# A hybrid decoder block on one core: norms taken by positions, a last sum moved ahead of scalings, and seven operand tiles loaded earlier

## The chip, the cores and the metric

The kernel runs on one core of a Trainium2 chip. The metric is the device time of one execution in microseconds (us), as the median of several runs. The engines of the core work beside each other, each through its own list of instructions in order: TensorE (PE in the profile; PEld is its loading of weights), VectorE (DVE), ScalarE (ACT), GpSimd (POOL), and SyncE (SP), which here only issues DMA transfers. Matmul results land in PSUM, where the kernel keeps eight buffers (banks) of 128 x 512 fp32.

## The reference

One layer of a decoder over 2048 positions and 1024 channels: a norm, an input projection, two mixers beside each other (gated linear attention and a short gated convolution), an output projection with a residual sum, a second norm, a gated FFN with 2816 inner channels and a residual sum, and a final norm. What the change touches are the second and the final norm and the end of the FFN:

```python
def rmsnorm(x, g):
    xf = x.astype(jnp.float32)
    y = xf * lax.rsqrt(jnp.mean(xf * xf, axis=-1, keepdims=True) + NORM_EPS)
    return (y * g.astype(jnp.float32)).astype(x.dtype)
...
        x = x + mixed
        h2 = rmsnorm(x, norm2_g[l])
        ffn = (jax.nn.silu(h2 @ w_ffn_gate[l]) * (h2 @ w_ffn_up[l])) @ w_ffn_down[l]
        x = x + ffn
    return rmsnorm(x, norm_f_g)
```

## The kernel before

**Layout.** Activations lie with channels on the 128 partitions and positions along the free dimension. The 2048 positions are four blocks of 512 (`PB`); two blocks, `j` = 0 and 1, form a half, and the kernel goes through the layer in two halves. 1024 channels are eight tiles (`d` or `k`). A tile is 128 x 512 fp32.

**Products.** fp32 accuracy is had from fp32r matmuls: `split` (L145 and L146) writes the rounded part of a tile on ACT and the rest of it on DVE, and `product_step` (L358 to L360) makes three matmuls for each pair of tiles. `unit` multiplies a 2 x 2 arrangement of blocks with seven products instead of eight (`PRODUCTS`); its weights are combined on POOL (L341 to L348) and split; its results are copied out of PSUM on ACT (L378) and added on DVE (L382). Operand pairs (`op`, 512 KB) lie in a pool `opp` of 28 buffers, raw weights in a pool of two, tiles of work beside the products in a pool of 11 (`bt`), split tiles on their way to DRAM (`so`) in a pool of 3.

**FFN.** For each half `ffn_up` runs over 11 pairs of row tiles: gate and up products, silu, product, and the split operands are stored to DRAM (`sa_...`) by a background generator. Then `ffn_down` sums over the 11 pairs in four groups (`GROUPS`: 2, 3, 3 and 3 pairs). For each group it loads 14 or 21 operand pairs (`act_op`, L137 on SP) and runs four units, each for two output tiles. The sums `y` of group 0 lie in 7 buffers of `opp`. The last unit of the second half is `last_unit`: four plain blocks of 18 matmuls, one for each of two tiles and two blocks of positions.

**Norms.** The sum of squares over the eight tiles is kept as a tile `ssq` of 128 x 512. `column_rstd` (L163) or `psum_rstd` (L170) multiplies it with a 128 x 128 matrix of ones, in plain fp32, so that every partition has the total (`tot`, PSUM). `finish_rstd` takes Ln (L176) and Exp (L177) on ACT, and one Newton step on DVE: L178, and L155 to L157 through `newton`. Scaled tiles follow on DVE (L482, L965, L992). ACT loads a table of functions when it goes from silu to Ln, from Ln to Exp, and back. There are eight such norms: two of the first half, taken while the second half's output projection runs (`h2_first`, near 714 us), two of the second half, taken beside the first half's `ffn_up` (`h2_ahead`, near 821 and 844), two final norms of the first half beside the second half's `ffn_up` (`finish_later`, near 1551 and 1730), and two at the end (`norm` in `last_unit`, L983 and L984, with the last tile's squares `q` as a second matmul).

**The end.** `last_unit` adds the last products to the sums (L1009), takes squares (ACT L1011), multiplies by the gains (L978), takes `norm(0)` ahead of the last 18 matmuls and `norm(1)` behind them, and scales block 0, then block 1 (L992): six tiles of each on DVE, two (`d` = 2 and 5) on POOL, which works from a copy of the norm in SBUF made by ACT (L986). Each scaled tile is stored (SP, L140).

**What sets the order.** The program is written once, in the order of the Python code; a planner with simulated times then fixes each engine's list when the kernel is built. `background` generators add norm and split work between products (`tick`). On the chip each engine keeps its list, whatever comes late.

## Time and profile before

| | |
|---|---|
| median of 3 runs | 2129.43 us (2121.35 to 2132.37) |
| profiled execution | 2130.55 us |
| its span | 2128.8 us |
| mean granted TensorE clock | 0.987 |
| PE busy | 2043.5 us, 96% |
| DVE, ACT, POOL busy | 1415.6, 1015.7, 971.7 us |
| DMA | 470.74 MB, mean 221 GB/s |

A line of the waits has the waiting engine, its instruction, what released it, and then the total in us, the number of waits and the longest. A line of the timeline has start, length, engine, source line and operation, output and inputs, a count where equal instructions are merged, and in brackets the idle time before it and what ended it. A line of the windows has the stretch, its length, the busy time and number of instructions of PE, PEld, DVE, ACT and POOL (or of one engine alone), then the granted clock, the DMA engines' share and GB/s. Where a tile or line is asked for, a line has the count, the shortest, median and longest duration in ns, and the first and last start. A line of the page's groups ends with busy time, mean ns and idle time before.

### The profile page before, as it was taken

The numbers are of one execution on the slowest core, as the hardware profiler recorded it, in microseconds if no ns is written. First come the engines' busy times: TensorE is split into PE (matmuls) and PEld (weight loads), VectorE is DVE, ScalarE is ACT, GpSimd is POOL, SyncE is SP. The second block draws the span as 40 slices with busy tenths as digits, with TensorE's granted clock in tenths as the row PEclk, the third lists the DMA queues.
The fourth block names the chain that finished last, engine by engine and source line by source line (L and its number), as shares of the span: only waits on it lengthen the run. The fifth ranks groups of instructions, "written<-read, shape, count | busy, mean of one in ns | idle before, by whom it ended". The sixth has DMA issues, their size and how long they took to land.

```text
span 2128.8 us, 26931 instructions
## 1 busy us (share of the span) xinstructions
PE 2043.5 (96%) x9133; PEld 1653.7 (78%) x9133; DVE 1415.6 (66%) x1983; ACT 1015.7 (48%) x1997; POOL 971.7 (46%) x703
## 2 busy tenths in 40 slices
PE   5999999999999999999999999999999989999996
PEld 4777787887888888788888877787888878886774
DVE  7668765549753695887886655654766666664554
ACT  5555445656543345545545443333554454453344
POOL 3435322222102464565464437864545545435774
PEclk9999999999999999999999999999999999999998
DMA  7349586424586872655646677697454535587662
GB/s 272 127 149 310 189 337 216 144 100 133 183 302 219 333 275 99 238 198 212 224 168 217 256 304 262 239 343 291 158 211 170 208 129 187 203 330 268 266 267 109
DMA packets 190971, 470.74 MB, mean 221 GB/s; under 512 B 20016, under 2 KB 65264, under 8 KB 181232
## 3 DMA queue, kind: packets, MB, share of 16 engines
q1 hardware_dynamic: 190832, 469.01, 60.6%
q8 instruction: 72, 1.18, 0.2%
q14 instruction: 67, 0.55, 0.1%
HBM read 300.63 MB, written 168.30 MB: 220 GB/s over the span
## 4 chain that ended last, share of the span: by engine, by line
PE 76%; DMA 10%; DVE 8%; ACT 3%; issue 2%; POOL 0%; SPq 0%; DVEq 0%; ACTq 0%; POOLq 0%
PE mm L358 22%; PE mm L360 22%; PE mm L359 21%; PE mm L776 2%; PE mm L777 2%; PE mm L779 2%; DMA raw<-in_wdown_dram 2%; DVE wq L146 2%; DMA op<-sa_T 1%; DMA op<-sa_B 1%; DMA op<-shT 1%; DVE so L146 1%; DVE op L146 1%; DMA h<-in_xt_dram 1%; DVE h L482 1%
## 5 line engine op out<-in xcount | busy, mean ns | idle before, releaser
L358 PE MATMUL mm<-op,wq 128*128 128x512 f32 x2499 | 985.4, 396 | 29.1 <-ACT c L378 9.8
L360 PE MATMUL mm<-op,wq 128*128 128x512 f32 x2499 | 970.4, 393 | 14.9 <-DVE wq L146 14.0
L359 PE MATMUL mm<-op,wq 128*128 128x512 f32 x2499 | 979.2, 392 | 0.0
L146 DVE TENSOR_TENSOR wq<-raw,wq 128x512 fp32r<-128x512 f32 (+2 forms) x626 | 524.6, 844 | 334.0 <-ACT wq L145 332.1
L145 ACT ACTIVATE wq<-raw 128x512 fp32r<-128x512 f32 (+2 forms) x626 | 364.8, 587 | 588.3 <-PE mm L360 421.2
L358 PEld LDWEIGHTS mm<-op,wq 128*128 128x128 f32 x2499 | 472.5, 189 | 147.8 <-ACT c L378 13.1
L360 PEld LDWEIGHTS mm<-op,wq 128*128 128x128 f32 x2499 | 472.5, 189 | 126.5 <-DVE wq L146 27.1
L359 PEld LDWEIGHTS mm<-op,wq 128*128 128x128 f32 x2499 | 472.9, 189 | 97.0 <-issue 1.0
L343 POOL TENSOR_TENSOR raw<-s,raw 128x512 f32<-128x512 f32 (+2 forms) x97 | 127.2, 1311 | 437.2 <-DVE wq L146 416.6
L382 DVE TENSOR_TENSOR c<-mm,c 128x512 f32<-128x512 f32 x267 | 182.8, 685 | 113.2 <-PE mm L360 109.9
L341 POOL TENSOR_TENSOR s<-raw 128x512 f32<-128x512 f32 (+2 forms) x97 | 127.3, 1313 | 196.5 <-DMA raw<-in_wffn_dram 90.3
L348 POOL TENSOR_TENSOR raw<-raw 128x512 f32<-128x512 f32 (+2 forms) x97 | 125.9, 1298 | 137.0 <-DVE wq L146 129.8
L378 ACT ACTIVATE c<-mm 128x512 f32<-128x512 f32 x267 | 154.4, 584 | 26.4 <-PE mm L360 23.9
L758 POOL TENSOR_TENSOR ssx<-ssx,q 128x512 f32<-128x512 f32 x52 | 76.2, 1477 | 159.8 <-ACT q L757 159.6
L342 POOL TENSOR_TENSOR raw<-raw 128x512 f32<-128x512 f32 (+2 forms) x97 | 136.8, 1411 | 4.4
L938 POOL TENSOR_TENSOR y<-c,y 128x512 f32<-128x512 f32 x66 | 99.1, 1504 | 68.9 <-DVE c L382 68.7
L146 DVE TENSOR_TENSOR so<-t,so 128x512 fp32r<-128x512 f32 x100 | 90.8, 914 | 19.0 <-ACT so L145 18.7
L145 ACT ACTIVATE wq<-s 128x512 fp32r<-128x512 f32 (+2 forms) x97 | 56.8, 586 | 92.7 <-PE mm L360 90.7
L776 PE MATMUL mm<-op,wq 128*128 128x512 f32 x256 | 100.9, 395 | 0.0
L777 PE MATMUL mm<-op,wq 128*128 128x512 f32 x256 | 99.8, 390 | 0.0
L146 DVE TENSOR_TENSOR wq<-s,wq 128x512 fp32r<-128x512 f32 (+2 forms) x97 | 86.1, 887 | 16.0 <-ACT wq L145 15.3
L145 ACT ACTIVATE so<-t 128x512 fp32r<-128x512 f32 x100 | 62.5, 628 | 44.2 <-DMA sa_B<-so 17.5
(175 smaller groups left out, 1882.2 us busy)
## 6 DMA issues: line engine op xcount, KB each, us to landing
raw<-in_wffn_dram SPq DMA_DIRECT2D x44, 1024.0 KB, 5.9
sa_T<-so SPq DMA_DIRECT2D x88, 512.0 KB, 5.0
op<-sa_T SPq DMA_DIRECT2D x88, 512.0 KB, 9.6
sa_B<-so SPq DMA_DIRECT2D x69, 512.0 KB, 3.4
op<-sa_B SPq DMA_DIRECT2D x69, 512.0 KB, 9.6
raw<-in_win_dram SPq DMA_DIRECT2D x23, 1024.0 KB, 5.3
raw<-in_wdown_dram SPq DMA_DIRECT2D x24, 768.0 KB, 6.1
sx<-y SPq DMA_DIRECT2D x48, 256.0 KB, 3.1
```

The source lines that it names most:

```text
L145: last_hi[:] = [act.activation(hi, src, AF.Copy)]
L146: return dve.tensor_tensor(lo, src, hi.bitcast(F32), ALU.subtract)
L341: pool.tensor_tensor(s1, a21, a22, ALU.add)
L342: pool.tensor_tensor(a21, a11, a21, ALU.subtract)
L343: pool.tensor_tensor(a11, s1, a11, ALU.subtract)
L358: pe.matmul(o[:], wh, xh, start=first and k == 0, stop=False, skip_group_check=True)
L359: pe.matmul(o[:], wh, xl, start=False, stop=False, skip_group_check=True)
L360: return pe.matmul(o[:], wl, xh, start=False, stop=k == n - 1, skip_group_check=True)
L378: act.activation(t[:], o[:], AF.Copy)
L382: dve.tensor_tensor(t[:], o[:], t[:], ALU.add)
L776: pe.matmul(o[e, j][:], wh, m[:, 0, :], start=k == 0, stop=False)
L777: pe.matmul(o[e, j][:], wh, m[:, 1, :], start=False, stop=False)
```

## The change

Three things change.

1. The norms after the first one go by positions (`position_rstd`). `ssq` becomes the stationary side of four matmuls with one column of ones, so that the totals of 512 positions come out as 128 x 4 in PSUM (`rs`). DVE computes the reciprocal root from a bit trick and three Newton steps on 128 x 4 elements, all without ACT; a copy on DVE spreads it to 128 x 512 (`rep`), and four transposes on PE give the row that every partition needs (`rb_ps`). At the end a second set of transposes goes to a bank of its own, for ACT's copy. Ln, Exp and their table loads go; `ident` moves to a pool that lives to the end.
2. At the end the last sum and its squares come ahead of block 0's scalings on DVE. Block 0's tiles 2, 5 and 6 go to POOL, 0 and 1 to DVE after the last sum, 3, 4 and 7 to DVE after the second norm's copy.
3. In `ffn_down`, seven (`EARLY`) of the 21 operand pairs of group 1 are loaded in the second unit of group 0, by the program's order, instead of after group 0.

```diff
-    ident = mixer.tile([P, P], F32, name="ident")
+    ident = const.tile([P, P], F32, name="ident")
...
-    def column_rstd(ssq, n, rb=None):
-    def psum_rstd(ssq, n):
-    def finish_rstd(v, tot, n, rb=None):
...
+    def position_rstd(n, *sums, into=()):
+        s, rb = bank("rs"), bank("rb_ps")
+        tot, v, l = [s[:, i * PT : (i + 1) * PT] for i in range(3)]
+        y = tiny.tile([P, PT], F32, name="py", tag="py")[:]
+        for t in range(PT):
+            for i, ssq in enumerate(sums):
+                pe.matmul(
+                    tot[:, t : t + 1], ssq[:, t * P : (t + 1) * P], one_t, start=i == 0,
+                    stop=i == len(sums) - 1,
+                )
+        dve.tensor_scalar(v, tot, 1.0 / n, EPS, ALU.mult, ALU.add)
+        li = l.bitcast(I32)
+        dve.tensor_scalar(li, v.bitcast(I32), 1, None, ALU.arith_shift_right)
+        dve.tensor_scalar(y.bitcast(I32), li, -1, 0x5F3759DF, ALU.mult, ALU.add)
+        for _ in range(3):
+            dve.tensor_tensor(l, v, y, ALU.mult)
+            dve.scalar_tensor_tensor(l, l, -0.5, y, ALU.mult, ALU.mult)
+            dve.scalar_tensor_tensor(y, l, 1.5, y, ALU.add, ALU.mult)
+        rep = bt("rep", (P, PT, P))
+        last_rep[:] = [
+            dve.tensor_copy(rep[:], y.rearrange("p (t c) -> p t c", c=1).to_broadcast([P, PT, P]))
+        ]
+        for dst in (rb, *into):
+            for t in range(PT):
+                pe.transpose(dst[:, t * P : (t + 1) * P], rep[:, t, :], ident[:])
         return rb
...
-            column_rstd(ssq[j], D, rb[j])
+            act.activation(rb[j][:], position_rstd(D, ssq[j])[:], AF.Copy)
...
-            rb.append(psum_rstd(ssq[j], D))
+            rb.append(position_rstd(D, ssq[j]))
...
+        def group_op(m, n):
+            return early.pop((m, n)) if (m, n) in early else act_op(half, m, n)
...
+                if u == 0 and d0 == 2:
+                    order = [(m, n) for _, n in PRODUCTS for m in range(GROUPS[1], GROUPS[2])]
+                    for m, n in order[:EARLY]:
+                        early[m, n] = act_op(half, m, n)
...
-            act.preload_act_table_set("natural_log_exp_and_others")
-            rb = psum_rstd(ssq, D)
+            rb = position_rstd(D, ssq)
...
         def norm(j, q):
-            tot, rb = bank("tot"), bank("rb")
-            pe.matmul(tot[:], ones[:], ssq[j][:], start=True, stop=False)
-            pe.matmul(tot[:], ones[:], q[:], start=False, stop=True)
-            finish_rstd(ssq[j], tot, D, rb)
-            act.activation(ssq[j][:], rb[:], AF.Copy)
+            copied = bank("rb_ps")
+            rb = position_rstd(D, ssq[j], q, into=[copied])
+            act.activation(ssq[j][:], copied[:], AF.Copy)
             return rb
...
-                dve.tensor_tensor(yy, o[:], yy, ALU.add)
+                added = dve.tensor_tensor(yy, o[:], yy, ALU.add)
...
                 if j and not r:
-                    rbs.append(norm(0, q[0]))
-        rbs.append(norm(1, q[1]))
-        for j in range(2):
-            scale(j, rbs[j])
+                    rb = norm(0, q[0])
+                    for d in (2, 5, 6):
+                        scale(0, d, None)
+        for d in (0, 1):
+            with tc.issue_after(added.ins):
+                scale(0, d, rb)
+        rb1 = norm(1, q[1])
+        for d in (3, 4, 7):
+            with tc.issue_after(last_rep[0].ins):
+                scale(0, d, rb)
+        for d in range(KD):
+            scale(1, d, None if d in (2, 5) else rb1)
```

More of the change, by code (lines that the diff above doesn't have):

```diff
@@ L13 @@
 U32 = mybir.dt.uint32
+I32 = mybir.dt.int32
 AF = mybir.ActivationFunctionType
@@ L30 @@
 LAST_GROUP = GROUPS[-1]
+EARLY = 7
 EPS = 1e-6
@@ L157, in newton @@
         dve.scalar_tensor_tensor(y, l, 1.5, y0, ALU.add, ALU.mult)
-    def column_rstd(ssq, n, rb=None):
-        rb = ssq if rb is None else rb
-        tot = bank("tot")
-        pe.matmul(tot[:], ones[:], ssq[:], start=True, stop=True)
-        finish_rstd(rb, tot, n)
-        return rb
-    def psum_rstd(ssq, n):
-        tot, rb = bank("tot"), bank("rb_ps")
-        pe.matmul(tot[:], ones[:], ssq[:], start=True, stop=True)
-        finish_rstd(ssq, tot, n, rb)
-        return rb
-    def finish_rstd(v, tot, n, rb=None):
-        l, y0 = bt("l"), bt("y0")
-        act.activation(l[:], tot[:], AF.Ln, bias=eps[:], scale=1.0 / n)
-        act.activation(y0[:], l[:], AF.Exp, scale=-0.5)
-        dve.tensor_scalar(v[:], tot[:], 1.0 / n, EPS, ALU.mult, ALU.add)
-        newton((v if rb is None else rb)[:], v[:], l[:], y0[:])
+    def position_rstd(n, *sums, into=()):
[23 more added lines that the diff above has]
+                pe.transpose(dst[:, t * P : (t + 1) * P], rep[:, t, :], ident[:])
+        return rb
+    last_rep = []
     background = []
@@ L903, in ffn_down @@
     def ffn_down(half):
-        y = {}
+        y, early = {}, {}
+        def group_op(m, n):
+            return early.pop((m, n)) if (m, n) in early else act_op(half, m, n)
         for u, m0 in enumerate(GROUPS):
@@ L910, in ffn_down @@
                 drain_background()
-            ops = {n: [act_op(half, m, n) for m in ms] for _, n in PRODUCTS}
+            ops = {n: [group_op(m, n) for m in ms] for _, n in PRODUCTS}
             if last and half:
@@ L973, in last_unit @@
         columns = (ops["B11"], ops["B21"]), (b12, ops["B22"])
-        with tc.issue_after(last_hi[0].ins):
-            act.preload_act_table_set("natural_log_exp_and_others")
         def gain(d, j):
@@ L980, in norm, with scale @@
         def norm(j, q):
-            tot, rb = bank("tot"), bank("rb")
-            pe.matmul(tot[:], ones[:], ssq[j][:], start=True, stop=False)
-            pe.matmul(tot[:], ones[:], q[:], start=False, stop=True)
-            finish_rstd(ssq[j], tot, D, rb)
-            act.activation(ssq[j][:], rb[:], AF.Copy)
-            return rb
-        def scale(j, rb):
-            for d in range(KD):
-                eng, by = (pool, ssq[j]) if d in (2, 5) else (dve, rb)
-                eng.tensor_tensor(y[d, j], y[d, j], by[:], ALU.mult)
-                store(out[2 + j, :, d, :], y[d, j])
+            copied = bank("rb_ps")
+            rb = position_rstd(D, ssq[j], q, into=[copied])
+            act.activation(ssq[j][:], copied[:], AF.Copy)
+            return rb
+        def scale(j, d, rb):
+            eng, by = (dve, rb) if rb is not None else (pool, ssq[j])
+            eng.tensor_tensor(y[d, j], y[d, j], by[:], ALU.mult)
+            store(out[2 + j, :, d, :], y[d, j])
         for d in range(KD - 2):
@@ L997, in last_unit @@
                 gain(d, j)
-        q, rbs = {}, []
+        q = {}
         for j in range(2):
```

## The prediction

> **What bounds the kernel now.** I read the page's first part, then the waits of PE, then PE's own matmuls counted in windows, then the timeline of each place that the change touches.

> ```profile
> PE 2043.5 (96%) x9133; PEld 1653.7 (78%) x9133; DVE 1415.6 (66%) x1983; ACT 1015.7 (48%) x1997; POOL 971.7 (46%) x703
> PE mm L358 <- DVE c L382: 7.7, 2, 7.0
> PE tot L984 <- ACT q L1011: 4.5, 1, 4.5
> PE mm L358 <- DMA op<-sa_T: 2.7, 8, 0.4
> PE mm L358 <- DMA op<-sa_B: 2.2, 7, 0.3
> ```

> TensorE has work in 96% of the span, so only time in which PE stands still, or its share of a chain that nothing covers, can be won. The waits name the places: one of 7.0 us behind DVE, one of 4.5 at the very end, and fifteen short ones for operand tiles. The short ones understate, because ends of matmuls are modelled; counting starts is better.

> ```profile
> 1725.62 0.39 PE L360 MATMUL mm<-op,wq 128*128 128x512 f32 x1
> 1728.34 0.39 PE L360 MATMUL mm<-op,wq 128*128 128x512 f32 x1
> 840.00:870.00 30.00, 26.56 (x112) 1.00 0.54 200
> 1255.00:1300.00 45.00, 41.09 (x165) 0.96 0.85 325
> 1720.00:1750.00 30.00, 22.66 (x90) 0.89 0.47 175
> 1910.00:1950.00 40.00, 35.71 (x139) 0.96 0.94 366
> ```

> Twelve matmuls lie between the first two rows: 2.72 us, 0.227 each. The other rows count the matmuls of `mm` alone in four stretches. 165 in 45 us need 37.4, so 7.6 are lost; 139 in 40 need 31.5, 8.5 lost; 90 in 30 need 20.4, and 0.9 goes to a norm's own matmul, 8.7 lost; 112 in 30 need 25.4 and 0.9, 3.7 lost. The two of 7.6 and 8.5 are the passage from row group 0 to row group 1 of the down projection, once in each half; 8.7 and 3.7 hold norms. The last number but two is the granted clock: 0.89 over 30 us is 6.6 us at half rate.

> **The change part by part.**

> *Seven tiles a group ahead.* Before, SP issues the 21 operand loads of group 1 in a row, late.

> ```profile
> 1215.63 13.02 SPq L140 DMA_DIRECT2D sa_B<-so  x3
> 1247.26 1.55 SPq L137 DMA_DIRECT2D op<-sa_B  x3
> 1220.00:1230.00 10.00, 10.00 (x46) 8.18 (x44) 8.79 (x11) 5.74 (x13) 7.16 (x6) 1.00 0.64 255
> 1240.00:1245.00 5.00, 5.00 (x23) 4.13 (x22) 2.20 (x4) 3.13 (x7) 2.45 (x3) 1.00 0.21 79
> 1270.00:1275.00 5.00, 3.85 (x12) 1.94 (x12) 0.69 (x1) 0.00 (x0) 1.87 (x2) 1.00 1.03 411
> 1278.43 0.52 ACT L145 ACTIVATE wq<-raw 128x384 fp32r<-128x384 f32 x1 [10.91 <-DMA raw<-in_wdown_dram]
> 1279.01 0.50 PE L358 MATMUL mm<-op,wq 128*128 128x512 f32 x1 [1.54 <-ACT wq L145]
> ```

> From 1220 to 1230 the DMA engines move 255 GB/s, at 1240 only 79; at 1270 they are full at 411, where a tile of 512 KB takes 1.28 us and PE uses it up in three matmuls, 0.68 us. Eight or so tiles at that difference of 0.6, the weights behind them in the same queue (1.54 us for PE) and the lower clock make up the 8 us. In the changed program's order on SP the seven loads stand after the first store of `sa_10`, that is at 1216 instead of 1247: they pass two stores of operands, two weight loads of the first group, four more stores and the first weight load of group 1. SP takes 13 us over three stores there, most of it waiting, so seven issues cost it nothing; the seven transfers are 9 us of DMA time, and they run on into stretches at 255 and 79 GB/s. The buffers are there: of 28, group 0 holds 14 and the sums 7. PE's unit before 1279 has 63 matmuls (14.3 us) and lost about 4, so it began group 1 at about 1259, and the 42 matmuls of group 0's last unit at about 1249.5. The other 14 tiles follow as that unit uses up group 0's, from about 1251, and end at 1251 + 14 x 1.28 + one weight load of 1.9 = 1271. PE needs the last at 1259 + 20 x 0.68 = 1272.5. So it just fits. Bounds: nothing won, or all 16.1 of both halves. I take 14, near the full end, because the sum above leaves only 1 us of slack: **-14**.

> *Norms by positions: what one costs.* A norm was a matmul over 512 columns, two ACT functions and four DVE operations over 512 columns. It becomes four sums of one column, twelve DVE operations over 4 columns, a copy to 128x512 and four transposes.

> ```profile
> 14.45 0.16 DVE L156 SCALAR_TENSOR_TENSOR rl<-rl,msq 128x4 f32<-128x4 f32 x1
> 14.65 0.16 DVE L157 SCALAR_TENSOR_TENSOR msq<-rl,ry 128x4 f32<-128x4 f32 x1
> L449 DVE COPY rep<-msq x16: 211/224/904, 14.8 to 108.3; 128x128 f32<-128x128 f32 x16
> L155 DVE TENSOR_TENSOR rl<-ry x4: 149/153/1246, 14.3 to 78.9; 128x4 f32<-128x4 f32 x4
> 410.11 0.38 PE L700 MATMUL o_ps<-vt,scores 128*128 128x128 f32 x2
> 410.32 0.39 PE L702 MATMUL o_ps<-carry,kq 128*128 128x128 f32 x2
> 404.18 0.60 PE L736 MATMUL ot<-ident,osb 128*128 128x128 f32 x4
> 2101.94 1.02 PE L983 MATMUL tot<-ssx,ones 128*128 128x512 f32 x2
> 2102.80 1.02 PE L984 MATMUL tot<-q,ones 128*128 128x512 f32 x2
> ```

> A DVE operation over 4 columns follows the last after 0.2 us: twelve are 2.3. The copy: 0.224 at 128 columns and 0.153 at 4 give 0.57 ns a column, 0.44 for 512. An fp32 matmul with 128 columns (two records) follows the last after 0.22; one with a single column isn't in the trace, and lies between nothing and that, so four are up to 0.9; I take 0.9. Four transposes: 0.45. PE gives 1.35 for 0.86 (the two rows of `tot`), +0.5 for each of six norms. Against it ACT loses its part altogether. [...]

> What matters more: PE takes its instructions in order, and the transposes wait for the copy. The changed program's order tells how many matmuls stand between the sums and the transposes as cover: 37 and 11 for the two norms of the output projection, 36 and 24 for those beside the first FFN unit, 24 and 12 for the two beside the second half's FFN, none for the first norm of the end.

> *Output projection.* The second norm has 11 matmuls, 2.5 us, and then its transposes. On DVE five of its twelve small steps stand before the four sums that close the column group, seven and a weight split between and behind them.

> ```profile
> 768.19 2.46 DVE L801 TENSOR_TENSOR y<-y,mm 128x512 f32<-128x512 f32 x4
> 799.18 0.50 PE L360 MATMUL mm<-op,wq 128*128 128x512 f32 x1 [2.12 <-DVE wq L146]
> L146 DVE TENSOR_TENSOR wq<-raw,wq 128x512 fp32r<-128x512 f32 (+2 forms) x626 | 524.6, 844 | 334.0 <-ACT wq L145 332.1
> ```

> Sums 2.46, split 0.84, seven steps 1.4, copy 0.44: 5.1 us, of which 1.3 can go ahead of the group's end, since its first two sums are complete six matmuls earlier. PE waits 4 us, comes back at half rate (+1.5), and has +1.0 of new work. All that DVE does for the next FFN starts 8 us later, and 2.1 us of waiting at 799.18 is there to meet it: it may vanish under the delay or stay. +6.5 less 1: **+5.5**, bounds 0 and +10.

> *Norms beside the FFN.* The last norm of the first half's output is where the 8.7 us are lost.

> ```profile
> 1734.94 1.28 ACT L176 ACT_TABLE_LOAD   x1
> 1739.92 1.28 ACT L414 ACT_TABLE_LOAD   x1
> 1740.02 0.68 DVE L382 TENSOR_TENSOR c<-mm,c 128x512 f32<-128x512 f32 x1
> 1740.76 0.80 PE L358 MATMUL mm<-op,wq 128*128 128x512 f32 x1 [7.05 <-DVE c L382]
> ```

> PE waits for DVE's sum at 1740.02, which stands behind a norm step that waits for ACT, and ACT switches tables three times (first and last shown). Without table loads ACT does its next split at 1734.9, DVE its half of it at 1735.6 and the sum at about 1736.2, and PE resumes at 1737 instead of 1740.8. Next late are the transposes: sum, one split, eleven steps and the copy end at 1740.3, PE has its 12 matmuls done at 1739.7. So 3.8 are won, 0.6 and 0.5 given back, and the half-rate stretch, of which 3.4 us lie behind 1740.8 (1.7 us), goes or stays: **-3.5**, bounds -8 and +1. The 3.7 us of 840 to 870 go partly the same way, less 1.0 of PE work: **-1**, bounds -3.5 and +2. The norm at 1551 loses nothing now: **+1**, bounds 0 and +4.

> *The end.* What is won: the last sum no longer stands behind six scalings.

> ```profile
> 2107.55 0.39 PE L360 MATMUL mm<-op,wq 128*128 128x512 f32 x1
> 2111.93 0.68 DVE L1009 TENSOR_TENSOR y<-mm,y 128x512 f32<-128x512 f32 x1
> 2113.33 2.07 PE L984 MATMUL tot<-q,ones 128*128 128x512 f32 x2 [4.53 <-ACT q L1011]
> 2119.63 3.67 DVE L992 TENSOR_TENSOR y<-y,rb 128x512 f32<-128x512 f32 x6 [0.66 <-ACT ssx L986]
> 2119.68 2.49 POOL L992 TENSOR_TENSOR y<-y,ssx 128x512 f32<-128x512 f32 x2 [8.80 <-ACT ssx L986]
> 2122.00:2124.00 2.00, 0.00 (x0) 0.00 (x0) 1.30 (x3) 0.00 (x0) 0.17 (x1) 0.50 1.02 380
> ```

> The last matmul is done at 2107.9, the sum starts at 2111.93: 4 us. But the first block's eight transposes now stand ahead of the last 18 matmuls. From 2101.94: sums 1.8, hand-over 0.2, steps and copy 2.7, transposes 0.9, then 18 x 0.227 = 4.1: the last matmul is done at 2111.9, the sum starts at 2112.0, and nothing is won there. After it: sum and square 1.4, column sums 1.7, hand-over 0.2, steps and copy 2.7, to 2118; three scalings left of the first block (1.8) and six of the second (3.7): 2123.5, against 2123.3 now. POOL's three scalings of the first block, 1.25 each, run before that, from 2108.9. The wait of 0.66 for ACT's copy goes, since that copy has a bank of its own. Stores: 11 tiles of 256 KB at 380 GB/s are 7.6 us against 5.5 for eight now, and start 1.6 sooner (2118 for 2119.63), so DMA is done 0.5 later. If the 2.9 us wait lowers the clock, 1.7 more. **+1.5**, bounds -1 and +5.

> Sum: -14 + 5.5 - 3.5 - 1 + 1 + 1.5 = -10.5. The profiled execution took 2130.55 us (span 2128.8), 1.1 over the median 2129.43 of the runs. **2120 us.**

> **The rivals.**

> *The norms turn into PE waits (slower).* All eight norms put transposes into PE's order. If DVE runs later than the cover, PE stands. For: between 1720 and 1750 DVE was late by 7 us, and the L155 row has 1246 ns for an operation of 153. Against: four norms have 24 to 37 matmuls, 5.4 to 8.4 us, for a chain of 2.7. It decides once DVE is over 5 us behind its place in most of them: eight waits of 3 us and 1.5 of half rate are +36, less 14 for the tiles and 3 where ACT is relieved: 2150 us. [...]

> *The norms cost nothing.* The output projection's wait is covered and the clock stays up: +1 there, -7 at 1740, 0 at the end: 2130.5 - 14 + 1 - 7 - 1 = 2110 us. For: ACT is relieved at every norm. Against: the order on DVE has four sums between the steps.

> *The loads only move the queue.* The seven transfers push stores and weight loads of group 0 back, and the passage keeps most of its loss: 10 of 14 lost, 2130 us, no change. For: 13 us of SP over three stores. Against: 79 GB/s at 1240.

> **How the numbers follow.** Forecast 0.50, with a range of its own of 2114 to 2125; free norms 0.22; moved queue 0.16; PE waits 0.12. No change is within 0.5%, 10.6 us, about what a measurement can tell here: 2118.8 to 2140 against the median. The forecast's middle lies just inside; with ACT relieved I give it 0.28 faster and 0.22 no change. Faster 0.28 + 0.22 = 0.50, same 0.22 + 0.16 = 0.38, slower 0.12. The range must reach free norms and moved queue: 2106 to 2133; only the slower case and an end of the free one, 0.15, lie outside.

> **What would show it.** Right: matmul counts of 1255 to 1300 and 1910 to 1950 near the 0.227 pace, granted clock 1.00, and no wait of ACT for `wdown` weights; a PE wait for the copy of about 4 us at 727; no 7 us wait near 1740; the last sum at about the same distance from the end. Wrong: new waits of PE before most transposes, or waits for `op` tiles that stay.

## The result and the profile after

The changed kernel takes 2134.06 us (median of 22 runs, 2128.41 to 2142.3); the kernel before, beside it, 2128.93 (22 runs). The ratio is 1.0029, 95% interval 1.0020 to 1.0039: 0.3% slower, inside the 0.5% that I called no change, but on the other side of the forecast of 2120 and 1 us above the range.

The page's first part, the waits of PE and the four windows of `mm` matmuls, all of the kernel after:

```profile
PE 2048.4 (96%) x9233; PEld 1664.5 (78%) x9233; DVE 1408.8 (66%) x2054; ACT 989.9 (46%) x1970; POOL 972.5 (46%) x704
```

```profile
PE mm L372 <- DVE wq L148: 15.1, 12, 3.5
...
PE rb_ps L188 <- DVE rep L184: 9.5, 3, 3.4
PE mm L370 <- ACT wq L147: 8.1, 8, 1.7
...
PE mm L370 <- DVE c L394: 2.6, 2, 1.9
...
PE mm L370 <- DVE y L394: 1.6, 2, 0.8
```

```profile
840.00:870.00 30.00, 28.97 (x126) 1.00 0.32 118
1255.00:1300.00 45.00, 44.33 (x194) 1.00 0.83 314
1720.00:1750.00 30.00, 27.34 (x112) 0.94 0.51 191
1910.00:1950.00 40.00, 39.85 (x175) 1.00 0.94 350
```

Where the change wanted to win, it did: the two passages have 194 and 175 matmuls instead of 165 and 139, the short waits for `op` tiles are gone, and the 7.0 us behind DVE near 1740 are 1.9. (The windows lie on each trace's own time; after is 7 to 15 us late in them, so 840 to 870 does not hold the same work in both.) The waits show what took their place: three for the copies of norms (9.5 us), stops for split weights, two behind `y` in group 0.

To see each place by itself I take the start of the n-th matmul of `mm` in one trace less that of the same matmul in the trace of before; both have 8361. The columns are times in the trace of before, the last one is the last matmul. Stretches that nothing touches drift by up to 5 us from run to run (most before 250 us, and around 1450), so only the step across a short stretch is read, and that too only to about 2 us: in the kernels that leave a place as it was, the steps are -1.0 to +1.7 from 735 to 815, -2.1 to +0.4 from 1195 to 1320 and -2.3 to -0.8 from 1860 to 1975.

```
                          716   735   790   815   870   915  1195  1320  1540  1600  1715  1765  1860  1975  2069  last
after                     0.0   7.0   8.3  12.3   9.2  11.9  11.7   7.1   7.8   9.3   9.3   4.5   4.5   1.9   0.7   6.8
loads alone (7)          -2.3  -2.3  -2.3  -2.3  -1.3  -1.5  -1.6  -6.2  -7.0  -6.7  -6.7  -6.8  -6.8 -10.8 -10.8 -10.5
loads alone (3)           1.1   1.1   1.1   2.4   3.4   3.2   4.4  -1.3  -2.0  -1.9  -1.9  -1.7  -1.7  -7.0  -8.3  -8.2
7 loads, third unit      -2.3  -2.3  -2.3  -3.3  -2.3  -2.5  -1.8  -6.3  -6.0  -6.0  -6.0  -5.6  -5.6  -8.5  -9.2  -9.2
output projection alone  -0.5   7.7   8.1  12.9  13.8  14.2  14.0  12.0  11.4  11.4  11.4  11.1  11.1  10.3   8.4   8.6
 ... late transposes     -2.3  -1.4  -1.4   3.9   4.9   5.8   5.7   3.6   0.4   1.0   1.0  -0.2  -0.2  -2.4  -3.9  -3.9
 ... and 3 us sooner     -1.2  -0.3  -0.3  -0.8   1.4   1.2   1.1   0.5  -3.3  -2.8  -2.8  -3.8  -3.8  -5.7  -7.4  -7.4
FFN norms alone          -1.6  -1.6  -1.6  -2.5  -5.4  -4.9  -5.1  -5.7  -6.1  -4.8  -4.8  -9.6  -9.6 -10.7 -11.7 -11.1
end alone                -3.5  -3.5  -3.5  -1.8  -0.8  -1.0  -0.8  -2.0  -3.3  -3.3  -3.3  -2.9  -2.9  -4.7  -5.0   1.7
 ... late transposes      0.1   0.1   0.1   1.5   1.4   2.2   2.1   2.3  -0.5  -0.5  -0.5   0.6   0.6  -0.2   0.1   0.6
old norms, empty steps   -1.1  -1.1  -1.1  -1.5  -1.5  -0.8  -0.7  -0.6  -1.1  -1.1  -1.1  -0.9  -0.9  -3.2  -4.7  -4.7
old norms, 12 steps      -1.3   0.5   0.5   8.8   9.8  11.0  10.9  11.3  10.6  10.6  10.6  11.0  11.0   8.8   7.1   7.2
old norms, 15 steps      -5.7  -3.9  -3.1   5.3   6.3   6.7   6.8   6.9   6.6   7.1   7.1   7.3   7.3   5.2   4.0   4.0
```

In the first row the output projection and the start of the FFN cost 12.3 us (716 to 815), the two groups win 4.6 and 2.6 (1195 to 1320, 1860 to 1975), the norms beside the FFN win 0.4 (815 to 915) and 4.8 (1715 to 1765) and cost 1.5 (1540 to 1600), and at the end the last matmul is 4.9 later. The span is 3.1 longer: what follows the last matmul is 3.7 shorter. The timeline of after shows the largest of them, in PE, DVE and SP, with two windows of the clock (last number but two) after the waits:

```profile
723.62 0.95 PE L170 MATMUL rs<-ones,ssx 128*128 128x1 f32 x8
724.61 0.17 DVE L174 TENSOR_SCALAR rs<-rs 128x4 f32<-128x4 f32 x1 [2.76 <-PE rs L170]
725.64 1.28 DVE L813 TENSOR_TENSOR y<-y,mm 128x512 f32<-128x512 f32 x2
...
729.82 0.69 DVE L184 COPY rep<-py 128x512 f32<-128x512 f32 x1
730.29 1.85 SPq L139 DMA_DIRECT2D h<-sx  x4
...
730.57 0.66 PE L188 MATMUL rb_ps<-ident,rep 128*128 128x128 f32 x4 [3.35 <-DVE rep L184]
...
735.06 2.15 DVE L494 SCALAR_TENSOR_TENSOR h<-h,sml,rb 128x512 f32<-128x512 f32 x3 [4.55 <-DMA h<-sx]
...
809.88 0.50 PE L372 MATMUL mm<-op,wq 128*128 128x512 f32 x1 [3.48 <-DVE wq L148]
```

```profile
732.00:734.00 2.00, 2.00 (x6) 1.61 (x5) 0.00 (x0) 0.00 (x0) 0.00 (x0) 0.51 0.91 310
...
811.00:813.00 2.00, 2.00 (x6) 1.52 (x6) 0.74 (x1) 0.63 (x1) 1.80 (x2) 0.50 0.00 0
```

The reader is to see three things: the column group's sums (L813) stand between the first and the last small step, so that the copy ends 5.9 us after the sums of one column; PE waits 3.35 for it and comes back at half rate (granted clock 0.51); and the first loads of `x1` (`h<-sx`) leave SP at 730.29, behind four stores of those sums (`sx<-y`, 726.36), where the kernel before issued them at 710.29.

```profile
710.29 8.71 SPq L137 DMA_DIRECT2D h<-sx  x7
719.86 1.41 DVE L482 SCALAR_TENSOR_TENSOR h<-h,sml,rb 128x512 f32<-128x512 f32 x2
```

These two rows are the kernel before: its first scaling runs at 719.86, that of after at 735.06, 15 us later.

### The profile page after: what moved, and what is told of

Its sections match the earlier page's. It is cut to its first block, busy times and chain, and to the rows that moved or that the text cites. A ratio compares the mean times of both kernels' runs of the same rounds, so it can differ in the third digit from the quotient of the medians.

```text
span 2131.9 us, 27186 instructions
## 1 busy us (share of the span) xinstructions
PE 2048.4 (96%) x9233; PEld 1664.5 (78%) x9233; DVE 1408.8 (66%) x2054; ACT 989.9 (46%) x1970; POOL 972.5 (46%) x704
## 4 chain that ended last, share of the span: by engine, by line
PE 72%; DVE 10%; DMA 9%; POOL 3%; issue 3%; ACT 2%; SPq 0%; DVEq 0%; ACTq 0%; POOLq 0%
PE mm L370 21%; PE mm L372 21%; PE mm L371 21%; DVE wq L148 2%; PE mm L788 1%; PE mm L789 1%; PE mm L791 1%; DVE so L148 1%; DVE op L148 1%; DVE h L494 1%; DMA raw<-in_win_dram 1%; DMA raw<-in_wdown_dram 1%; DMA op<-shT 1%; POOL y L959 1%; DMA raw<-in_wffn_dram 1%
## 5 line engine op out<-in xcount | busy, mean ns | idle before, releaser
L370 PE MATMUL mm<-op,wq 128*128 128x512 f32 x2499 | 982.5, 395 | 25.6 <-ACT c L390 11.3
L372 PE MATMUL mm<-op,wq 128*128 128x512 f32 x2499 | 968.4, 393 | 16.0 <-DVE wq L148 15.1
L371 PE MATMUL mm<-op,wq 128*128 128x512 f32 x2499 | 978.1, 391 | 0.0
L355 POOL TENSOR_TENSOR raw<-s,raw 128x512 f32<-128x512 f32 (+2 forms) x97 | 128.0, 1320 | 441.3 <-DVE wq L148 404.9
L360 POOL TENSOR_TENSOR raw<-raw 128x512 f32<-128x512 f32 (+2 forms) x97 | 125.3, 1292 | 136.4 <-DVE wq L148 129.1
L788 PE MATMUL mm<-op,wq 128*128 128x512 f32 x256 | 101.2, 397 | 0.0
L789 PE MATMUL mm<-op,wq 128*128 128x512 f32 x256 | 100.3, 392 | 0.0
L148 DVE TENSOR_TENSOR wq<-s,wq 128x512 fp32r<-128x512 f32 (+2 forms) x97 | 81.8, 843 | 17.4 <-ACT wq L147 16.7
L791 PE MATMUL mm<-op,wq 128*128 128x512 f32 x256 | 80.7, 394 | 1.0 <-DVE wq L148 1.0
```

What stands on the lines that cost most here:

```text
L148: return dve.tensor_tensor(lo, src, hi.bitcast(F32), ALU.subtract)
L355: pool.tensor_tensor(a11, s1, a11, ALU.subtract)
L360: pool.tensor_tensor(a12, a12, a11, ALU.subtract)
L370: pe.matmul(o[:], wh, xh, start=first and k == 0, stop=False, skip_group_check=True)
L371: pe.matmul(o[:], wh, xl, start=False, stop=False, skip_group_check=True)
L372: return pe.matmul(o[:], wl, xh, start=False, stop=k == n - 1, skip_group_check=True)
```

## The experiments

All ratios are to the kernel before, run beside each kernel on the same chip.

| kernel | median us | before us | ratio, 95% interval |
|---|---|---|---|
| seven loads alone | 2121.96 | 2126.66 | 0.9979 (0.9967 to 0.9991) |
| output projection alone | 2137.26 | 2126.66 | 1.0043 (1.0028 to 1.0059) |
| FFN norms alone | 2120.29 | 2126.66 | 0.9973 (0.9962 to 0.9983) |
| end alone | 2129.04 | 2126.66 | 1.0015 (1.0005 to 1.0026) |
| all but the output projection | 2120.88 | 2128.40 | 0.9962 (0.9950 to 0.9974) |
| output projection, late transposes | 2128.20 | 2128.40 | 1.0011 (0.9998 to 1.0023) |
| the same, 3 us sooner | 2124.26 | 2126.51 | 0.9988 (0.9977 to 1.0000) |
| end, late transposes | 2124.63 | 2128.40 | 0.9982 (0.9971 to 0.9993) |
| seven loads, third unit | 2121.58 | 2128.40 | 0.9974 (0.9963 to 0.9985) |
| three loads | 2117.47 | 2129.51 | 0.9950 (0.9931 to 0.9970) |
| old norms, empty steps behind | 2127.82 | 2126.51 | 1.0001 (0.9991 to 1.0011) |
| old norms, 12 steps in front | 2137.64 | 2125.63 | 1.0058 (1.0039 to 1.0077) |
| old norms, 15 steps in front | 2135.70 | 2125.63 | 1.0047 (1.0030 to 1.0064) |
| whole change, late transposes | 2119.07 | 2129.51 | 0.9954 (0.9938 to 0.9970) |
| old output projection, rest late | 2114.57 | 2129.51 | 0.9930 (0.9910 to 0.9950) |
| the same, loads in the third unit | 2112.89 | 2129.51 | 0.9926 (0.9907 to 0.9945) |
| the same, three loads | 2111.59 | 2126.51 | 0.9930 (0.9918 to 0.9942) |
| whole change, all steps at their best | 2112.45 | 2126.51 | 0.9931 (0.9917 to 0.9944) |

**Each part alone.** Four kernels put one part of the change into the kernel before.

```diff
# loads alone: column_rstd and psum_rstd at every norm, the old end, and only
+                if u == 0 and d0 == 2:
+                    for m, n in order[:EARLY]:
+                        early[m, n] = act_op(half, m, n)
# output projection alone: EARLY = 0, and only
+            act.activation(rb[j][:], position_rstd(D, ssq[j])[:], AF.Copy)
# FFN norms alone: EARLY = 0, and only
+            rb.append(position_rstd(D, ssq[j]))     # h2_ahead
+            rb = position_rstd(D, ssq)              # finish_later
# end alone: EARLY = 0, and only last_unit as changed
```

> The seven early loads alone, with the norms and the end of the kernel before. Theory A (each part keeps its own price, and they add up): the passage from group 0 to group 1 gains about 8 us in each half, and the transfers stop PE at two places late in group 0 (about 1252 and 1256, 0.8 and 1.5 us before the clock), 3 us each time, so -9 to -10 us in all, 0.9955 of the time before. Rival B (the two stops in group 0 come from the order that the norms by positions bring about, not from the loads): no stops in group 0, -16 us, 0.9925. Rival C (the forecast's term): -14.

> Norms by positions in the output projection alone. Theory A: the wait of about 3.4 us for the copy near 730, the half-rate stretch behind it and new stalls near 773, 806 and 810, because DVE is late with all that follows: +11 to +13 us at 870, 1.0055 of the time before. Rival B (the new stalls between 770 and 815 belong to the norms beside the FFN, whose steps are drawn out of the same background): only the wait near 730, +5 to +7 us. The forecast's term was +5.5.

> Norms by positions only beside the FFN (the two of the second half and the two final ones of the first half). Theory A: about 0 between 830 and 910, +2 near 1551, -5 near 1740: -3 us, 0.9985. Rival B (the stalls of 770 to 815 belong to these norms): +5 us by 815 and -5 at 1740, no change. The forecast's terms were -1, +1 and -3.5.

> The end alone: norms by positions and the last sum ahead of the scalings. Theory A: PE waits 3 us for the first norm's copy ahead of the last 18 matmuls, comes back at half rate, and the end is 2 to 3 us later: 1.001. Rival B (the gain of the moved sum is real, and the changed kernel's end is late only because of what came before): -2 us, 0.999. The forecast's term was +1.5.

The four ratios add up to +0.10%, the changed kernel has +0.29; the intervals of four parts are wide enough for that. All but the output projection gives 0.9962, against -0.33% from its three parts, so no meeting of parts is needed to explain the result:

```diff
-            act.activation(rb[j][:], position_rstd(D, ssq[j])[:], AF.Copy)
+            column_rstd(ssq[j], D, rb[j])
```

> The whole change but for the output projection, whose two norms are taken as in the kernel before. Theory A (the +12 us between 716 and 810 belong to those two norms alone, and the parts add up: loads -0.2%, FFN norms -0.3%, end +0.15%): 0.9965 of the time before, -7 us. Rival B (the parts meet, and the changed kernel is late by more than the sum of its parts for a reason outside the output projection): 0.999 or more.

The loads alone win 4.6 and 4.0 us at the passages in the trace, 8.6 against theory A's 9 to 10, but their time, 0.9979, is half the gain that theory A expected (0.9955). The output projection alone loses 13.4 us between 716 and 815, with the same wait of 3.4 and the same stall at 809.89. The FFN norms alone lose nothing at 815 and win 8.0 from 716 to 1765 (3.3 by 915, 4.8 at 1740, less 1.3 at 1551, the rest drift): theory A for both parts, and for the FFN norms more than its -3. The end alone has the 6.4 us late last matmul and the 3.7 us shorter rest, which is theory A's 2 to 3 us.

**The loads.** The timeline of the kernel with seven loads alone, SP, POOL and PE:

```profile
1227.67 0.33 SPq L139 DMA_DIRECT2D raw<-in_wdown_first_dram  x1
...
1237.24 0.74 POOL L375 TENSOR_TENSOR s<-raw 128x256 f32<-128x256 f32 x1 [4.78 <-DMA raw<-in_wdown_first_dram]
...
1239.15 0.50 PE L392 MATMUL mm<-op,wq 128*128 128x512 f32 x1 [0.79 <-DVE y L416]
...
1242.33 0.50 PE L392 MATMUL mm<-op,wq 128*128 128x512 f32 x1 [1.51 <-ACT wq L147]
```

In the kernel before, POOL uses the same weight tile without a wait, 5.7 us after its issue at 1229.24:

```profile
1234.91 0.92 POOL L341 TENSOR_TENSOR s<-raw 128x256 f32<-128x256 f32 x1
```

The weight tile issued behind the seven is used by POOL 9.6 us later, after POOL has stood 4.8 us for it, and PE stops twice, at the two places where the changed kernel stops too (1252.47 and 1255.64, 0.78 and 1.51). So the stops belong to the loads, not to the norms. Two sizes of the cause:

```diff
-EARLY = 7
+EARLY = 3
# the other kernel: seven loads, one unit later
-                if u == 0 and d0 == 2:
+                if u == 0 and d0 == 4:
```

> Three early loads instead of seven, alone, in the second unit of group 0. Theory A (the two stops near 1239 and 1242 come from a weight load that lands 4.8 us late behind seven tiles of 1.28 us each): three tiles delay it by 5 us less, the stops of 0.8 and 1.5 us go, and the passage keeps 7 - 3 = 4 tiles of its old lateness, some 4 us: -3 to -5 us in each half at the passage, with no loss ahead of it. Rival B (the stops come from the order of POOL's and ACT's work, which the planner lays out anew with any early load): the stops stay.

> The seven early loads alone, but issued in the third unit of group 0 instead of the second. Theory A (the two stops of 0.8 and 1.5 us near 1239 and 1242 come from a weight load that stands behind the seven transfers at full DMA rate): with the seven behind that weight load the stops go, the passage keeps its gain of 8, and the group gives -8 us in each half, 0.9925 of the time before. Rival B (a later issue collides with the weight loads of the last unit, or comes too late for group 1): stops at another place, or a passage that loses 3 us or more again: 0.996 to 0.998.

With three loads the same rows read:

```profile
1233.90 0.33 SPq L139 DMA_DIRECT2D raw<-in_wdown_first_dram  x1
...
1238.65 0.73 POOL L375 TENSOR_TENSOR s<-raw 128x256 f32<-128x256 f32 x1 [0.27 <-DMA raw<-in_wdown_first_dram]
```

The weights land within 4.7 us, POOL waits 0.27, both stops are gone, and the passages win 5.7 and 5.3 (1195 to 1320, 1860 to 1975), where seven loads win 4.6 and 4.0. That is theory A; the excess over its 3 to 5, and the 1 us more than with seven, are within the drift of these stretches. In time three loads stand at 0.9950 and seven at 0.9979, with intervals that just overlap. In the third unit the seven win 4.5 and 2.9: the 1.51 stop goes, the one of 0.8 moves to 1248, and POOL waits 7.35 us for the next weight tile. That was rival B: seven tiles are in front of some weight load wherever they stand.

**The output projection: the transposes' place.** The work is the same; both norms' sums and steps stand together, and the transposes 33 matmuls behind the sums in the trace.

```diff
         for j in range(2):
+            spread.append(position_rstd(D, ssq[j], later=True))   # sums, steps, copy
+            yield
+        for j in range(2):
+            row, wide = spread[j]
+            for t in range(PT):
+                pe.transpose(row[:, t * P : (t + 1) * P], wide[:, t, :], ident[:])
             rb.append(tiny.tile([P, PB], F32, name="rb2", tag="rb"))
-            act.activation(rb[j][:], position_rstd(D, ssq[j])[:], AF.Copy)
+            act.activation(rb[j][:], row[:], AF.Copy)
             yield
```

> Norms by positions in the output projection alone, as before, but both blocks' sums and small steps stand together, and the eight transposes stand 37 products behind the sums. The work is the same. Theory A (the loss is the place of the second norm's transposes in PE's order, 11 products behind their sums): no wait for the copy near 730, no half-rate stretch, +2 us of PE's own work by 735, and DVE, which is no longer parted from its norm by the group's sums, is not late at 800: +1 to +3 us by 870, 1.001. Rival B (the loss is DVE's own work or lateness): the stalls near 806 and 810 stay, +6 us or more by 870.

Both were half right. The wait near 730 is gone, and 716 to 735 costs 0.9 instead of 8.2. But 790 to 815 still loses 5.3. The timeline of this kernel, DVE and PE:

```profile
721.31 2.74 DVE L518 SCALAR_TENSOR_TENSOR h<-h,sml,rb 128x512 f32<-128x512 f32 x4 [1.70 <-ACT rb L857]
...
761.36 1.78 DVE L518 SCALAR_TENSOR_TENSOR h<-h,sml,rb 128x512 f32<-128x512 f32 x1
```

```profile
796.91 0.50 PE L394 MATMUL mm<-op,wq 128*128 128x512 f32 x1 [1.69 <-ACT wq L147]
801.13 0.80 PE L396 MATMUL mm<-op,wq 128*128 128x512 f32 x1 [3.48 <-DVE wq L148]
```

The last scaling still starts 5.4 us later than in the kernel before, whose sixteen start from 719.9 to 756.0:

```profile
L482 DVE SCALAR_TENSOR_TENSOR h<-h,sml,rb x16: 736/1396/1786, 719.9 to 756.0; 128x512 f32<-128x512 f32 x16
```

To tell lateness from the norms' own work I took the same norms sooner, and the old norms later.

```diff
# the same norms, sooner                  # kernel before, old norms later
-        for _ in range(6):
+        for _ in range(1):               # +        for _ in range(12):    (or 15)
             yield
# kernel before, empty steps behind the old norms
+        for _ in range(11):
+            yield
         yield from combine(lambda k, j: s_x1[j][k][:], C_G2, rb, put)
```

> The kernel before with one thing changed: eleven empty steps of the background between the two norms of the output projection and the first scaling behind them, about 15 us, as far as the scalings moved in the changed kernel (from 719.9 to 735.1). No norm by positions is in it. Theory A (the 4 to 5 us lost between 790 and 815 come from the late start of the scalings, which make DVE and ACT late with the first FFN operands and weights, whatever norm stands ahead): 3 to 5 us lost between 790 and 815, and nothing ahead of it; 1.002 of the time before. Rival B (they come from the new norms' own work, copies or banks): nothing lost, 1.000.

> The output projection alone with late transposes, as in the run with both norms together, but the norms begin five background steps sooner, which puts the sums and transposes about 3 us ahead. Theory A: the scalings start 3 us sooner, at about 718, and of the 5.3 us lost between 790 and 815 some 3 are won back: 2 to 3 us lost in all, 1.000. Rival B (the loss doesn't hang on when the scalings start): 5 us lost there as before.

> The kernel before with one thing changed: its two old norms in the output projection begin twelve background steps after the start instead of six, which puts their matmuls about 28 instructions later on TensorE and the first scaling behind the column group's sums, near 729 instead of 720. No norm by positions is in it. Theory A (what the start of the FFN loses, 4 to 5 us between 790 and 815, comes from the late start of the scalings): 2 to 5 us lost there, 1.001 to 1.0025 of the time before. Rival B (it comes from the new norms themselves): nothing lost there.

> The same with fifteen steps: the first scaling near 735, as late as in the changed kernel. Theory A: 4 to 6 us lost between 790 and 815, and more than with twelve. Rival B: nothing lost there.

The empty steps did not move the first scaling (718.8, with the whole trace 1.1 us early there) and the last by 1.8 us only: that run tells nothing about the cause. The other three do. Three us sooner, the new norms lose nothing between 790 and 815 (-0.5; expected were 2 to 3). The old norms, with no position norm in the program, lose 8.3 and 9.2 from 735 to 815 when they are late; with twelve steps that is more than theory A's 2 to 5, and the time, 1.0058, is above its 1.001 to 1.0025. The first of these, DVE and PE:

```profile
732.99 1.40 DVE L516 SCALAR_TENSOR_TENSOR h<-h,sml,rb 128x512 f32<-128x512 f32 x2
```

```profile
801.86 0.80 PE L392 MATMUL mm<-op,wq 128*128 128x512 f32 x1 [4.77 <-ACT wq L147]
806.07 0.79 PE L394 MATMUL mm<-op,wq 128*128 128x512 f32 x1 [3.00 <-DVE wq L148]
```

Counted against PE's own shift at 735, the last scaling starts 1.8 us late with the empty steps, 2.8 with the sooner norms, 5.4 in the output projection alone, 6.3 in the changed kernel, 6.7 with late transposes, 13 and 19 with the old norms late; the losses from 735 to 815 are -0.4, -0.5, 5.2, 5.3, 5.3, 8.3 and 9.2. So the start of the FFN takes about 3 us of lateness free and then pays, whichever norm causes it. The way it goes shows in ACT and SP. Part of the scaled tiles is stored to DRAM and loaded again (`h<-sfB`, `h<-sfT`) to be split into operands; the kernel before, then late transposes:

```profile
780.27 0.38 SPq L137 DMA_DIRECT2D h<-sfB  x1
...
788.23 0.63 ACT L145 ACTIVATE op<-h 128x512 fp32r<-128x512 f32 x1 [2.06 <-PE mm L779]
```

```profile
782.71 0.50 SPq L139 DMA_DIRECT2D h<-sfB  x1
...
790.77 0.63 ACT L147 ACTIVATE op<-h 128x512 fp32r<-128x512 f32 x1 [5.98 <-DMA h<-sfB]
```

Between 775 and 806 ACT stands for these loads not at all in the kernel before, 1.5 and 1.6 us in the two kernels that lose nothing, 4.3 in the output projection alone, 4.5 in the changed kernel, 6.3 with late transposes, 7.6 and 7.5 with the old norms late. No run holds the engines' order fixed: the planner also lays out DVE's and ACT's lists behind 740 anew in each of these kernels, so what the order adds stays open.

With fifteen steps the loss is above theory A's 4 to 6, and in the time of the whole kernel it is no slower than with twelve.

**The end.** The first norm's sums and steps stay ahead of the last 18 matmuls, its transposes go behind them.

```diff
-                    rb = norm(0, q[0])
-                    for d in (2, 5, 6):
-                        scale(0, d, None)
+                    rb, rep0 = position_rstd(D, ssq[0], q[0], later=True)
+                    copied0 = bank("rb_ps")
+        with tc.issue_after(done.ins):
+            for dst in (rb, copied0):
+                for t in range(PT):
+                    pe.transpose(dst[:, t * P : (t + 1) * P], rep0[:, t, :], ident[:])
+        act.activation(ssq[0][:], copied0[:], AF.Copy)
+        for d in (2, 5, 6):
+            scale(0, d, None)
```

> The end alone, with the first norm's eight transposes behind the last 18 products of TensorE instead of ahead of them; sums and small steps stay ahead. Theory A (the 6 us lost between 1945 and the last product are the wait of 3 us for the first norm's copy and the half rate behind it, with 1.7 us of transposes): the last product starts 5 to 6 us sooner than with the end of the changed kernel, and the last store 2 to 3 sooner: 0.999 to 1.000 of the time before. Rival B (the end is set by the last sum, the second norm and eleven stores, which come after the last product whatever stands ahead): the second norm now waits behind the first one's transposes, and nothing is won, 1.0015.

The timeline of after, PE and DVE, with the window of the clock, and then that of this experiment:

```profile
2108.24 1.97 PE L188 MATMUL rb_ps<-ident,rep 128*128 128x128 f32 x8 [3.17 <-DVE rep L184]
...
2114.80 0.69 DVE L1023 TENSOR_TENSOR y<-mm,y 128x512 f32<-128x512 f32 x1 [6.62 <-PE mm L372]
...
2120.73 5.46 DVE L1006 TENSOR_TENSOR y<-y,rb_ps 128x512 f32<-128x512 f32 x9
```

```profile
2108.00:2112.00 4.00, 3.76 (x15) 3.40 (x16) 0.18 (x1) 0.60 (x1) 1.02 (x1) 0.62 0.01 2
```

```profile
2108.53 0.69 DVE L1048 TENSOR_TENSOR y<-mm,y 128x512 f32<-128x512 f32 x1 [0.47 <-PE mm L396]
...
2109.61 1.09 PE L1060 MATMUL rb_ps<-ident,rep 128*128 128x128 f32 x8 [1.12 <-DVE rep L184]
...
2115.38 5.46 DVE L1031 TENSOR_TENSOR y<-y,rb_ps 128x512 f32<-128x512 f32 x9
```

In after PE stands 3.17 us, works at half rate (granted clock 0.50 from 2108 to 2110, 0.62 over the 4 us of the window), and the last sum starts at 2114.80 (before: 2111.93). Behind the matmuls the transposes wait 1.1 us, the last sum starts 6.3 sooner and the nine last scalings 5.3. Some 2.1 of both was there by 1975; counted from that place, the sum starts 4.1 sooner than in after, the scalings 3.2 and the end comes 3.1 sooner (than in the end alone 5.7, 4.8 and 4.7). About 1 us of what the sum gains goes to the second norm, which now waits behind the first one's transposes; the rest reaches the end. The last matmul is 0.8 later than the kernel before instead of 6.4 or 4.9 (from 1975). Theory A: 0.9982 against 1.0015 for the end alone; in the trace 2.0 us are won from 1975 to the end against the kernel before, which is its 0.999.

**Together.** Five kernels join the parts, in the places found above.

```diff
# whole change, late transposes: both edits above
# old output projection, rest late: column_rstd in h2_first, the end's edit, seven loads
# the same with d0 == 4, and the same with EARLY = 3
# whole change at its best: both edits, range(1), EARLY = 3
```

> The whole change, with two sets of transposes later: the output projection's eight stand 37 products behind their sums, and the first norm of the end has its eight behind the last 18 products. Theory A (the changed kernel is slower only by where these transposes stand; the parts as measured alone add up: loads -0.21%, FFN norms -0.27%, output projection +0.11%, end -0.18%): -0.55%, 0.9945 of the time before, and 0.9916 of the changed kernel. Rival B (parts meet, as the +0.29% of the changed kernel against a sum of +0.10% for its parts hints): 0.997 or more.

> The change with the output projection's norms as in the kernel before and the end's first transposes behind the last 18 products. Theory A (adding up): -0.21, -0.27 and -0.18%: 0.9934. Rival B (norms by positions are worth having everywhere once their transposes stand late, so that this one lacks something): slower than the whole change with late transposes.

> As the one with the old output projection and the late transposes at the end, but with the seven loads in the third unit of group 0. Theory A (one stop of 0.8 us is left instead of two of 0.8 and 1.5): 0.993, at most 1 us from the other. Rival B (the loads' place doesn't matter, since the passage loses later what the stops give back): the same time within 0.05%.

> The old norms in the output projection, norms by positions elsewhere, the late transposes at the end, and three early loads. Theory A: 3 us better than the same with seven loads in the second unit: 0.9915 to 0.9925. Rival B (the loads' number doesn't matter): 0.993.

> The whole change with its steps where the runs so far were best: the output projection's norms together, sooner and with late transposes, the end's first transposes behind the last 18 products, and three early loads instead of seven. Theory A (parts add up: three loads -11 us at the two passages, FFN norms -0.27%, end -0.18%, output projection +2 us): about 0.9925. Rival B: no better than the whole change with late transposes and seven loads, 0.9954.

The whole change with only the transposes moved is 0.46% faster than before, where the change as it came is 0.29% slower: theory A within its interval, with rival B's 0.997 at the interval's end. The other four, 0.9926 to 0.9931, beat the kernel before by 0.7% and the changed one by 1.0% (0.993 / 1.0029), and can't be told apart: seven loads, three, or seven in a later unit, old norms in the output projection or new ones taken soon enough. So joined with the rest, the number of loads makes no difference that these intervals can show: the measured 0.9930 is rival B's 0.993, and theory A's 0.9925 lies in the interval too. In the traces the stops and passages differ all the same.

## Why the prediction was wrong

Term by term, from the first row of the table of shifts:

| term | forecast | bounds | measured |
|---|---|---|---|
| seven loads | -14 | -16.1 to 0 | -7.2 (-4.6, -2.6) |
| output projection | +5.5 | 0 to +10 | +12.3 |
| norms near 821 and 844 | -1 | -3.5 to +2 | -0.4 |
| norm near 1551 | +1 | 0 to +4 | +1.5 |
| norm near 1740 | -3.5 | -8 to +1 | -4.8 |
| end | +1.5 | -1 to +5 | +1.2 (4.9 - 3.7) |

Two terms failed, by 6.8 us each, together the 13.6 between the forecast of -10.5 and the span's +3.1; the other four are off by 1.3 or less and nearly cancel. These are steps of one profiled execution each. By the medians the output projection alone costs 9.1 us (6.0 to 12.5), and the loads alone win 4.5 (1.9 to 7.0): the same two terms fail, the first by less and the second by more.

*Output projection.* The step that failed is "All that DVE does for the next FFN starts 8 us later, and 2.1 us of waiting at 799.18 is there to meet it: it may vanish under the delay or stay". The first half of the term was near: a wait of 3.35 for 4, half rate at 732 to 734, and +7.0 by 735 for 6.5. No run shows the 1.5 us that the forecast, and the rival of waits, set down for a return at half rate; in after the granted clock is 0.50 from 732.05 to 735.46, 1.7 us lost. But DVE's work for the FFN starts 15 us later: it stands behind the second norm, and then DVE waits 4.55 us more for loads that had moved 20 us in SP's order. I followed PE's and DVE's instructions there and not SP's. The wait did not vanish, it grew to 0.80 and 3.48 with half rate behind it (granted clock 0.50 from 811 to 813). The old norms taken late, and the new ones taken sooner, show that the loss comes with this lateness, whichever norm stands there; what the engines' changed order adds is open. In the traces the term is above my upper bound of +10; by the medians that bound lies inside its interval.

*Loads.* The step that failed is "seven issues cost it nothing; the seven transfers are 9 us of DMA time, and they run on into stretches at 255 and 79 GB/s". By the same count of matmuls the passages themselves won 8.1 and 8.9 (from 1246 to 1290 and 1918 to 1945), above the 7 a half that I took; 3.3 and 4.0 were lost ahead of them, and 2.3 behind the second, with a stop of 1.74 us at 1960.39 that no run takes apart. Part of the 8.1 and 8.9 is luck: in the trace of before both passages were followed by half rate (granted clock 0.50 from 1281 to 1283 and from 1939 to 1942), but in the ten traces without early loads only seven and four were, and where they were not the step without any loads is -1.1 to -2.3. A mean of GB/s says nothing of the one transfer that stands right behind: a weight tile kept POOL waiting 4.8 us with the loads alone, and 5.42 in after. The rival "the loads only move the queue" named that mechanism; by the trace its 10 of 14 lost were too much (6.8), by the medians not (9.5), and with three loads the stops are gone.

*What held.* The norm's price on each engine (twelve steps at 0.2 us, copy 0.43, four transposes 0.60 in the trace), the wait near 1740 and the norms beside the FFN; of the eight norms three made PE wait for a copy, 9.5 us in all, so the rival that had most of them do so did not come. At the end the sum was right, with the half rate that I had only named as possible (0.50 from 2108 to 2110): counted from 1975 the last matmul came 4.9 us later than before, and the last sum, which starts 0.43 us behind the start of that matmul instead of 4.38, gave 4.0 of it back. From the sum to the end it takes 17.1 us instead of 16.9, so the new norm itself gave nothing.

## What to carry to other kernels

When a step moves in an engine's order, follow the first DMA that its successor needs, not only its own engine: here two norms cost 12 us in the trace, of which 5 fell 70 us further on, because loads and scalings stood behind them. An early load has to be priced by the transfer behind it in the queue; three tiles fitted in front of a weight tile (POOL stood 0.27 us for it) and seven did not (4.78), though in the time of the whole change the two can't be told apart. Instructions for which an engine stands, as PE did here 3.35 and 3.17 us at transposes, belong behind the work that can cover them: moving two sets of transposes turned +0.3% into -0.5% with no work removed.

## What was not expected

*Where the clock falls.* In after, stops of 1.51 and 2.61 us leave the clock at full rate, and one of 1.92 halves it. The timeline of PE and the windows behind each:

```profile
1255.64 0.50 PE L370 MATMUL mm<-op,wq 128*128 128x512 f32 x1 [1.51 <-ACT wq L147]
...
1744.82 0.50 PE L370 MATMUL mm<-op,wq 128*128 128x512 f32 x1 [1.92 <-DVE c L394]
...
2067.56 0.50 PE L370 MATMUL mm<-op,wq 128*128 128x512 f32 x1 [2.61 <-ACT c L390]
```

```profile
1256.00:1260.00 4.00, 3.97 (x18) 2.95 (x17) 3.37 (x7) 1.93 (x6) 2.74 (x4) 1.00 0.67 263
...
1746.00:1748.00 2.00, 2.00 (x6) 1.52 (x5) 1.71 (x9) 0.00 (x0) 1.50 (x2) 0.50 1.03 422
1748.00:1750.00 2.00, 2.00 (x10) 1.57 (x9) 0.00 (x0) 0.54 (x2) 1.11 (x1) 0.70 0.98 384
...
2068.00:2071.00 3.00, 3.00 (x15) 2.47 (x14) 0.23 (x1) 1.57 (x3) 2.61 (x3) 1.00 0.68 262
```

*Two chains in one.* In the output projection with late transposes the two norms' steps alternate on DVE; first and last of the 24:

```profile
712.28 0.16 DVE L174 TENSOR_SCALAR rs<-rs 128x4 f32<-128x4 f32 x1
...
715.07 0.16 DVE L181 SCALAR_TENSOR_TENSOR py<-rs,py 128x4 f32<-128x4 f32 x1
```

24 steps and one copy take 2.95 us, 0.12 each, where one chain alone takes 0.20 a step. By these paces I estimate that in one chain alone some 0.08 us of each 0.20 is time that the steps of another chain can fill.
